# A hybrid attention block: PSUM as one tile with banks taken in turn by hand, and another order of steps at the last block's end

## The chip, the cores and the metric

The kernel runs on one core of one Trainium2 chip. The metric is the time of one execution on the device in microseconds (us). Its engines are named as in the profile: PE (TensorE, matmuls), DVE (VectorE), ACT (ScalarE), POOL (GpSimd) and SP (SyncE, here a queue for DMAs). PSUM, where matmuls leave their sums, has eight banks; one bank holds 128 rows of 512 fp32 numbers.

## The reference

One layer of a flow-matching backbone over 512 latent tokens of width 2048, with 256 context tokens:

```
h  = rmsnorm(x) * (1 + scale) + shift           # shift, scale, gate = silu(c) @ w_ada + b_ada
hc = the same of the context tokens
p  = h @ w_in                                   # 512 x 9216: q, k, v, z_a, u_b, z_b, g_a, g_b
q, k = rope(rmsnorm(heads)); kc, vc from hc @ w_in[:, k and v]
attn = softmax(q k^T) v                         # 12 heads over 4 k/v heads, 768 keys
y_a = (attn * silu(z_a)) @ w_proj_a
y_b = (fourier_2d(u_b) * silu(z_b)) @ w_proj_b
y   = (sigmoid(g_a) * y_a + sigmoid(g_b) * y_b) @ w_out
out = rmsnorm(x + gate * y) * final_g
```

All in fp32.

## The kernel before

Every fp32 product is made of three matmuls on halves of the numbers: each operand is split into a high part ("hi", rounded, by ACT, L163) and a low part ("lo", the difference, by DVE, L164), and `mm3` (L309) issues high times high, high times low and low times high (L311, L312, L313). The order of instructions on each engine is made by a planner, which models the time and takes, on each engine, the first instruction in program order whose inputs are ready; where the kernel says `issue_after` or `manual_schedule` it keeps the order written.

The stages, in order:

1. The start (to about 150 us): the modulation vectors (L492, a matrix-vector product whose weights are loaded while it runs), the normed tokens, and the products for the Fourier branch (`start_work`). It takes PSUM banks from a pool `ps` by three functions: `bank` (four buffers), `bank2` (two) and `bank3` (two). The Fourier transforms (`channels`, `positions`) use `bank`.
2. The projection groups (about 170 to 820 us): eight groups, of kinds qz, qz, qz, gate, gate, kv, gate, gate. A group makes a block of 1024 columns for all 512 tokens by seven products of a fast matrix scheme in place of eight: P1, Q5, P2, Q6, P7, Q3, Q4, in this order. A product comes in four pieces of weights, each with 12 matmuls, so 48 in all. P1 and P2 add up in one sum ("a"), Q5, Q6 and Q3 in a second ("b"), P7 and Q4 in a third ("c"). Each sum is a pair of banks. The second PSUM pool, `psp`, has two pairs under the tag "x" (for "a" and "c") and the pairs "y0" and "y1" (for "b"), taken by `pair`. The work at the end of a product takes pairs as well: in a qz group `pair("y")` at L906, `pair("x")` at L901 after P7 and `pair("y")` at L901 after Q3; in the kv group `pair("x")` at L916 after P2. At the end of Q4, DVE subtracts the sum "c" and the kept Q5 (L795, in `Group.run` L824), and the next group begins with P1. By Q5 of each group DVE also adds two loaded parts of its weights (L246).
3. Attention and the branch products (about 820 to 1180 us). Here the third pool, `psq`, is opened after `psp` is closed: one tile of all eight banks, with parts of it used by hand. `wide` are four stretches of one and a half banks over banks 0 to 5 for scores and transposes, bank 6 is for the `filler` (products that stand between those of the attention), bank 7 for the rest. Its first use is `fill(2)`: six matmuls into bank 6, then the first scores into `wide[1]`, that is the second half of bank 1 and bank 2.
4. The output projection (to the end): two groups of the same seven products. In the last one Q4 is done by `finish`: first the rows t=0, then t=1. For t=1 the last two of eight steps are done in column halves. `last` then weighs the sum with the gate, adds it to the rest, squares it with a running sum, and takes the root for the last norm; `Rms.scale` scales the four chunks of 512 columns and stores them.

A tile's users wait for each other by bank where it lies in PSUM. A new tile in a closed pool's place waits for all users of what lay there.

## Time and profile before

| | |
|---|---|
| median of 3 runs | 1321.96 us (1321.64 to 1322.66) |
| profiled execution | 1322.68 us |
| its span, first to last instruction | 1320.9 us |
| PE busy | 1297.7 us, 98% |
| DVE busy | 974.7 us, 74% |
| ACT busy | 652.7 us, 49% |
| POOL busy | 140.5 us, 11% |
| mean granted PE clock | 0.998 |

The span lies within the execution's time; 1.8 us lie around it. A line such as L313 is that of the helper `mm3`, so it stands for matmuls of all stages; what tells them apart is the name of the tile written: "pb", "pc", "pd" in the first pool, "x" and "y" in the second, "banks" in the third. In a timeline row the columns are the start and the length in us, the engine, the line, the operation, output<-inputs, the shape and the count, and in brackets the idle time before it and what ended it.

### The profile page before, as it was taken

What the parts mean: (1) busy time and instruction counts of PE and PEld (TensorE: products, weight loads), DVE (VectorE), ACT (ScalarE), POOL (GpSimd) and SP (SyncE); (2) the same over time, 40 slices, a digit from 0 to 9 for tenths busy, and PEclk for the clock granted to TensorE, in tenths of its full rate; (3) what the DMA queues carried; (4) which work ended last, traced back from release to release, by engine and by line L of the source; (5) the groups of instructions that cost most, each with busy time, mean ns of one, the idle gap of its engine ahead of it and who ended that gap; (6) DMA issues with size and microseconds to landing.
All of it is one profiled execution on the core that took longest, in us unless ns stands there. A gap on an engine that the chain in (4) does not pass through costs nothing.

```text
span 1320.9 us, 17489 instructions
## 1 busy us (share of the span) xinstructions
PE 1297.7 (98%) x6600; PEld 1062.3 (80%) x6600; DVE 974.7 (74%) x1290; ACT 652.7 (49%) x1019; POOL 140.5 (11%) x192
## 2 busy tenths in 40 slices
PE   7999999999999999999999999999999999999997
PEld 3577888888888888888888887888888888888885
DVE  4666899888777867746487666677776789777676
ACT  5222655555555554444354454666666133355544
POOL 0110011110201111011021110000000100111210
PEclk9999999999999999999999999999999999999999
DMA  9898587887898988977669886122013899678985
GB/s 382 330 371 340 175 243 196 226 233 219 205 318 196 276 280 244 297 166 190 193 167 303 235 245 217 45 72 81 33 65 112 321 332 329 186 175 222 225 208 170
DMA packets 96085, 291.28 MB, mean 221 GB/s; under 512 B 8960, under 2 KB 32000, under 8 KB 91648
## 3 DMA queue, kind: packets, MB, share of 16 engines
q1 hardware_dynamic: 48576, 163.65, 35.5%
q0 software_dynamic: 22800, 96.49, 30.7%
q10 hardware_dynamic: 24624, 30.02, 6.6%
q8 instruction: 52, 0.85, 0.3%
q14 instruction: 33, 0.27, 0.1%
HBM read 263.37 MB, written 26.75 MB: 220 GB/s over the span
## 4 chain that ended last, share of the span: by engine, by line
PE 96%; DMA 1%; ACT 1%; DVE 1%; issue 0%; SPq 0%; DVEq 0%; ACTq 0%
PE banks L311 11%; PE banks L312 11%; PE banks L313 11%; PE x L312 9%; PE x L313 9%; PE x L311 9%; PE y L312 8%; PE y L311 8%; PE y L313 8%; PE banks L1201 3%; PE pd L492 2%; PE pb L311 2%; PE pb L313 1%; PE pb L312 1%; PE pc L311 1%; PE pc L313 1%
## 5 line engine op out<-in xcount | busy, mean ns | idle before, releaser
L163 ACT ACTIVATE whi<-wr 128x1024 fp32r<-128x1024 f32 (+1 forms) x129 | 135.1, 1051 | 161.5 <-PE banks L313 91.8
L164 DVE TENSOR_TENSOR wlo<-wr,whi 128x1024 fp32r<-128x1024 f32 (+1 forms) x129 | 155.8, 1211 | 53.8 <-ACT whi L163 53.5
L164 DVE TENSOR_TENSOR wlo<-R,whi 128x1024 fp32r<-128x1024 f32 x114 | 138.5, 1221 | 65.7 <-ACT whi L163 65.4
L163 ACT ACTIVATE whi<-R 128x1024 fp32r<-128x1024 f32 x114 | 120.3, 1059 | 131.5 <-PE x L313 37.2
L311 PE MATMUL banks<-whi,s 128*128 128x512 f32 (+1 forms) x422 | 166.2, 394 | 1.7 <-DVE ev L795 1.5
L312 PE MATMUL banks<-wlo,s 128*128 128x512 f32 (+1 forms) x422 | 165.0, 391 | 0.0
L313 PE MATMUL banks<-whi,s 128*128 128x512 f32 (+1 forms) x422 | 164.5, 390 | 0.0
L311 PE MATMUL x<-whi,s 128*128 128x512 f32 x352 | 137.2, 390 | 0.0
L313 PE MATMUL x<-whi,s 128*128 128x512 f32 x352 | 137.0, 389 | 0.0
L312 PE MATMUL x<-wlo,s 128*128 128x512 f32 x352 | 137.0, 389 | 0.0
L311 PE MATMUL y<-whi,s 128*128 128x512 f32 x316 | 123.1, 389 | 0.0
L312 PE MATMUL y<-wlo,s 128*128 128x512 f32 x316 | 123.0, 389 | 0.0
L313 PE MATMUL y<-whi,s 128*128 128x512 f32 x316 | 122.8, 389 | 0.0
L267 POOL DMA_DIRECT2D R<-in_w_g x64 | 55.3, 865 | 421.5 <-DVE wlo L164 224.0
L163 ACT ACTIVATE s<-wr 128x512 fp32r<-128x512 f32 (+2 forms) x93 | 61.3, 678 | 65.9 <-PE y L312 16.3
L311 PEld LDWEIGHTS banks<-whi,s 128*128 128x128 f32 x422 | 79.3, 188 | 17.8 <-ACT whi L163 1.9
L313 PEld LDWEIGHTS banks<-whi,s 128*128 128x128 f32 x422 | 79.3, 188 | 16.3
L312 PEld LDWEIGHTS banks<-wlo,s 128*128 128x128 f32 x422 | 79.4, 188 | 14.8
L164 DVE TENSOR_TENSOR s<-wr,s 128x512 fp32r<-128x512 f32 (+2 forms) x93 | 67.1, 747 | 22.0 <-ACT s L163 20.8
L311 PEld LDWEIGHTS x<-whi,s 128*128 128x128 f32 x352 | 66.1, 188 | 13.7
L312 PEld LDWEIGHTS x<-wlo,s 128*128 128x128 f32 x352 | 66.1, 188 | 13.7 <-DVE wlo L164 0.2
L313 PEld LDWEIGHTS x<-whi,s 128*128 128x128 f32 x352 | 66.1, 188 | 13.6
(279 smaller groups left out, 2766.4 us busy)
## 6 DMA issues: line engine op xcount, KB each, us to landing
wr<-in_w_g SPq DMA_DIRECT2D x128, 512.0 KB, 5.1
R<-in_w_g POOLq DMA_DIRECT2D x64, 512.0 KB, 6.7
wa<-in_w_ss POOLq DMA_DIRECT2D x26, 1024.0 KB, 8.0
R<-in_w_g SPq DMA_DIRECT2D x32, 512.0 KB, 5.4
wr<-in_w_pab SPq DMA_DIRECT2D x32, 512.0 KB, 5.3
wr<-in_w_gate SPq DMA_DIRECT2D x32, 512.0 KB, 5.7
wr<-in_w_o SPq DMA_DIRECT2D x24, 512.0 KB, 6.7
R<-in_w_o POOLq DMA_DIRECT2D x24, 512.0 KB, 8.1
```

What stands on the lines that cost most here:

```text
L163: first = nc.scalar.activation(hi, src, ACT.Copy)
L164: return first, nc.vector.tensor_tensor(lo, src, hi.bitcast(F32), op=ALU.subtract)
L267: nc.gpsimd.dma_start(chain[e.pc], e.nxt, accum_op=ALU.add)
L311: nc.tensor.matmul(o, ah, bh, start=start, stop=False, skip_group_check=cont)
L312: nc.tensor.matmul(o, ah, bl, start=False, stop=False, skip_group_check=cont)
L313: nc.tensor.matmul(o, al, bh, start=False, stop=stop, skip_group_check=cont)
L492: last = nc.tensor.matmul(acc[32 * j : 32 * j + 32, :256], c2[:, kk, :], w[:, k, :], start=kk < 4, stop=kk >= KK - 4)
L1201: nc.tensor.transpose(tp[:, k * P : (k + 1) * P], p[:, k * P : (k + 1) * P], ident)
```

## The change

PSUM becomes one tile of eight banks, `whole_psum`, at the start of the kernel. `bank`, `bank2` and `bank3` take banks 0 to 3, 4 to 5 and 6 to 7 of it, each in strict turn. `pair` takes pairs in strict turn too, "x" from banks 0 to 3 and "y" from banks 4 to 7, where the second pool had tags with buffers. The closing of the first two pools goes. In `finish`, t=1 is done like t=0, in whole widths. In `last`, the weighing is one instruction for 512 columns; for t=1 the sum over the squares leaves out the last one (`rest`), which goes into the root as its input (`root_of`), with the sum of the others as its bias; and chunk 3 is scaled and stored in two halves (`scale_part`).

```diff
-    pss, ps = region("ps", None, space=PSUM)
+
+    psq = ctx.enter_context(tc.tile_pool(name="psq", bufs=1, space=PSUM, reuse_waits="tile"))
+    whole_psum = psq.tile([P, 8, 512], F32, name="banks")
+    turn_b = [0, 0, 0]
+
+    def next_bank(i, first, n):
+        turn_b[i] += 1
+        return whole_psum[:, first + (turn_b[i] - 1) % n, :]
...
-    def bank(shape=(P, 512)):
-        return ps.tile(list(shape), F32, tag="b1", bufs=4, name=uid("pb"))
+    def bank():
+        return next_bank(0, 0, 4)
 
     def bank2():
-        return ps.tile([P, 512], F32, tag="b2", bufs=2, name=uid("pd"))
+        return next_bank(1, 4, 2)
 
     def bank3():
-        return ps.tile([P, 512], F32, tag="b3", bufs=2, name=uid("pc"))
+        return next_bank(2, 6, 2)
...
-    pss.close()
...
-    pgs, psp = region("psp", None, space=PSUM, reuse_waits="tile")
-    last_y = [0]
-
-    banks = []
+    last_y = [0, 1]
...
     def pair(tag, skip=0):
-        if banks:
-            last_y[tag == "x"] += 1
-            b = 2 * (last_y[tag == "x"] % 2) + (4 if tag == "y" else 0)
-            return banks[0][:, b : b + 2, :] if b < 6 else banks[1]
-        if tag == "y":
-            last_y[0] += 1 + skip
-            return psp.tile([P, 2, 512], F32, tag=f"y{last_y[0] % 2}", bufs=1, name=uid(tag))
-        return psp.tile([P, 2, 512], F32, tag=tag, bufs=2, name=uid(tag))
+        last_y[tag == "x"] += 1 + skip
+        b = 2 * (last_y[tag == "x"] % 2) + (4 if tag == "y" else 0)
+        return whole_psum[:, b : b + 2, :]
...
             w = []
             for t in range(2):
-                for j in range(8 - 2 * t):
+                for j in range(8):
...
                     self.mm(a, form, j, t, w[j // 2], False, j == 7, cont=True)
-                if t:
-
-                    for c in (slice(0, 256), slice(256, 512)):
-                        for j in (6, 7):
-                            ah, al = (v[:, P:] for v in self.forms[form][j])
-                            mm3(a[:, t, c], ah, al, w[3][0][:, j % 2, c], w[3][1][:, j % 2, c], False, j == 7, cont=True)
                 self.last(self.Y, a, t)
...
-    pgs.close()
-    psq = ctx.enter_context(tc.tile_pool(name="psq", bufs=1, space=PSUM, reuse_waits="tile"))
-    whole_psum = psq.tile([P, 8, 512], F32, name="banks")
-    banks += [whole_psum[:, :6, :], whole_psum[:, 6:, :]]
+    banks = [whole_psum[:, :6, :], whole_psum[:, 6:, :]]
     last_y[:] = [0, 0]
...
+        def rest(self):
+            nc.vector.tensor_reduce(self.r[:, 0:1], ssq[:, self.t, 0:4], axis=AX.X, op=ALU.add)
+            nc.vector.tensor_scalar(self.r[:, 0:1], self.r[:, 0:1], 1.0 / D, EPS, op0=ALU.mult, op1=ALU.add)
+
+        def root_of(self, i):
+            nc.scalar.activation(self.r[:, 1:2], ssq[:, self.t, i : i + 1], ACT.Sqrt, bias=self.r[:, 0:1], scale=1.0 / D)
+
+        def scale_part(self, j, parts):
+
+            v, r = o[self.t // 2, j][:, self.t % 2, :], self.r[:, 1:2]
+            for c, _ in parts:
+                nc.scalar.mul(v[:, c], v[:, c], r)
+                nc.sync.dma_start(out[self.t * P : (self.t + 1) * P, 512 * j + c.start : 512 * j + c.stop], v[:, c])
...
-        def weigh(c):
-            nc.vector.tensor_tensor(tmp[:, c], a[:, t, c], gates[0][:, 0, c], op=ALU.mult)
-
-        def add(c, i):
-            nc.vector.tensor_tensor(Y[:, t, c], tmp[:, c], Y[:, t, c], op=ALU.add)
-            squares_of(Y[:, t, c], 2 + t, i)
-
         r = Rms(2 + t)
         with tc.manual_schedule(engines={mybir.EngineType.DVE, mybir.EngineType.Activation}):
+            nc.vector.tensor_tensor(tmp, a[:, t, :], gates[0][:, 0, :], op=ALU.mult)
             for c, i in half:
-                weigh(c)
-                add(c, i)
-            r.add()
-            r.root()
+                nc.vector.tensor_tensor(Y[:, t, c], tmp[:, c], Y[:, t, c], op=ALU.add)
+                squares_of(Y[:, t, c], 2 + t, i)
+            if t:
+
+                r.rest()
+                r.root_of(4)
+            else:
+                r.add()
+                r.root()
             r.turn()
-            r.scale(3, True)
+            if t:
+                r.scale_part(3, half)
+            else:
+                r.scale(3, True)
             r.scale(1)
```

## The prediction

> **What bounds the kernel now.** I read the page first (busy shares and the chain), then the waits of TensorE, then the windows by stage, then the timeline at the places that the change touches.

> ```profile
> PE 1297.7 (98%) x6600; PEld 1062.3 (80%) x6600; DVE 974.7 (74%) x1290; ACT 652.7 (49%) x1019; POOL 140.5 (11%) x192
> ...
> PE 96%; DMA 1%; ACT 1%; DVE 1%; issue 0%; SPq 0%; DVEq 0%; ACTq 0%
> ```

> TensorE is busy for 98% of the span and is 96% of the chain that ended last. So a stall of TensorE costs its length, and only what it waits for now can be won. The waits of TensorE, and the windows (columns: length; busy us of PE, PEld, DVE, ACT, POOL with counts; granted clock; DMA share; GB/s):

> ```profile
> PE banks L311 <- DVE ev L795: 1.5, 1, 1.5
> ```
> ```profile
> 25.00:140.00 115.00, 114.45 (x838) 76.53 (x837) 72.77 (x142) 31.88 (x48) 14.15 (x26) 1.00 0.87 337
> 240.00:815.00 575.00, 575.00 (x2544) 475.98 (x2544) 416.25 (x496) 288.54 (x465) 70.49 (x81) 1.00 0.82 233
> 815.00:840.00 25.00, 23.53 (x135) 20.10 (x134) 14.88 (x23) 13.80 (x21) 0.53 (x1) 1.00 0.29 108
> 840.00:1060.00 220.00, 218.72 (x1381) 189.56 (x1380) 163.65 (x268) 124.30 (x214) 10.53 (x20) 1.00 0.32 111
> 1311.60:1315.20 3.60, 0.00 (x0) 0.00 (x0) 2.50 (x7) 1.90 (x6) 0.00 (x0) 1.00 0.70 261
> 1315.30:1320.90 5.60, 0.00 (x0) 0.00 (x0) 0.72 (x2) 0.64 (x2) 0.00 (x0) 0.50 0.51 187
> ```

> From 240 to 815 us (the projection groups) TensorE never idles: 2544 matmuls in 575 us, 0.226 us from one to the next, so a product of 48 takes 10.85 us. The PSUM pools cost one visible wait, 1.5 us, where the third pool opens at 820 us. The first stage loses 0.55 us in 115 with DMA at 0.87, so by-hand banks have little to win there.

> **The change part by part.**

> *The pool boundary at 820 us.* One tile from the start means that a matmul waits for the last readers of its own bank, not of all eight.

> ```profile
> 819.83 0.39 PE L313 MATMUL x<-whi,s 128*128 128x512 f32 x1
> 821.69 0.47 PE L311 MATMUL banks<-whi,s 128*128 128x512 f32 x1 [1.47 <-DVE ev L795]
> 822.00 0.40 PE L312 MATMUL banks<-wlo,s 128*128 128x512 f32 x1
> 822.23 0.40 PE L313 MATMUL banks<-whi,s 128*128 128x512 f32 x1
> ```
> ```profile
> 820.26 1.29 DVE L795 TENSOR_TENSOR ev<-x,ev 128x512 f32<-128x512 f32 x2 [0.40 <-PE x L313]
> ```

> Unhindered, the third matmul would start at 819.83+3x0.226=820.51 instead of 822.23: 1.72 us are lost, of which 0.09 is the slow restart (0.54 for two steps instead of 0.45). After the change the first six matmuls (the filler, bank 6) wait for nothing, since bank 6 held the "b" sum that ended with Q3. They take 1.36 us, to 821.42. The scores that follow write the second half of bank 1 and bank 2; of these only bank 2 holds the sum of Q4, and its half of the subtraction is done by about 820.9. So the wait goes. What is late next is the softmax:

> ```profile
> 823.05 1.28 ACT L1185 ACT_TABLE_LOAD   x1 [0.41 <-ACT ev L850]
> 825.41 0.91 ACT L1185 ACTIVATE s<-banks,gain 128x768 f32<-128x768 f32 x1 [1.08 <-DVE gain L1183]
> ```

> The table load hangs on ScalarE's own queue and ends at 824.33 whatever TensorE does, so the first exponential moves by 825.41-824.33=1.08 us at most. Gain between 1.08 and 1.72; I take 1.5, since the later stage idles only 1.28 us in 220 and so has matmuls to put in between.

> *The turn of the "x" pairs.* Before, "x" is a tag with two buffers and a sum gets the one that is free; "y" alternated by name already. After, "x" strictly alternates too: odd turns are banks 2-3, even ones 0-1. Counting calls in a "qz" group: the "a" sum of P1 (turn 2, banks 0-1), the "c" sum of P7 (turn 3, banks 2-3), the tanh of the second half at L901 (turn 4, banks 0-1). Three are an odd number, so P1 of the next group is turn 5: banks 2-3, where the "c" sum of the Q4 just ended still waits for DVE's subtraction at L795. The same happens from the second to the third group and from the third to the first "gate" group. "gate" groups take two turns, the "kv" group three of which the last is P7's own, so it is not met again. Now the three places as they are:

> ```profile
> 248.15 1.22 DVE L795 TENSOR_TENSOR ev<-x,ev 128x1024 f32<-128x1024 f32 x1
> ...
> 323.78 1.22 DVE L795 TENSOR_TENSOR ev<-x,ev 128x1024 f32<-128x1024 f32 x1
> ...
> 400.18 1.22 DVE L246 TENSOR_TENSOR R<-R,wr 128x1024 f32<-128x1024 f32 x1
> 401.32 1.22 DVE L795 TENSOR_TENSOR ev<-x,ev 128x1024 f32<-128x1024 f32 x1
> 402.46 1.21 DVE L164 TENSOR_TENSOR wlo<-R,whi 128x1024 fp32r<-128x1024 f32 x1
> ```
> ```profile
> 248.21 0.39 PE L313 MATMUL x<-whi,s 128*128 128x512 f32 x1
> ...
> 257.95 0.39 PE L311 MATMUL y<-whi,s 128*128 128x512 f32 x1
> ...
> 334.11 0.39 PE L311 MATMUL y<-s,s 128*128 128x512 f32 x1
> ...
> 410.27 0.39 PE L311 MATMUL y<-whi,s 128*128 128x512 f32 x1
> ```

> The "y" rows are the first matmuls of Q5, so P1 began 10.85 us earlier: 247.10, 323.26, 399.42. At 248.21 it writes "x" while DVE reads "x": it has the other buffer. In the strict turn it starts when the subtraction has ended, with the 0.14 us between DVE's end (821.55) and the matmul (821.69) at the pool boundary, and the restart of 0.09. The losses are 249.37+0.23-247.10=2.50, 325.00+0.23-323.26=1.97 and 402.54+0.23-399.42=3.35, in all 7.8 us. The subtraction does not come at once because DVE is at other work (L246 in the third case). If it did, it would start 0.43 us after the last matmul's start, as at 820.26, and each stall would be 0.43-0.23+1.22+0.23=1.65, three 4.95 us.

> What could stand in the stall? Everything behind P1 on TensorE: matmuls of Q5's first piece write "y" and could go ahead.

> ```profile
> 399.65 1.06 ACT L163 ACTIVATE whi<-R 128x1024 fp32r<-128x1024 f32 x1 [1.67 <-PE x L313]
> ```
> ```profile
> 138.39 0.39 PE L311 MATMUL pc<-s,whi 128*128 128x512 f32 x1
> 138.83 1.21 PE L311 MATMUL pb<-s,whi 128*128 128x512 f32 x4
> ```

> That single matmuls are put ahead where others wait is seen at 138.39. But Q5's weights get their buffer only when Q4 is done (ScalarE waits for "PE x L313"), the high part is ready at 400.71 and the low part at 403.67, behind the subtraction. So the first matmul for each of two banks can go ahead, 0.45 us a stall. Bounds of the cost: 4.95-1.35=3.6 and 7.8. I take 7.8-1.35=6.5, as the rows of the three places themselves are the nearest. The stalls come in a stretch with no idle time, so nothing behind gives them back.

> A long stall could also cost clock. In the windows above TensorE has nothing to do from 1311.6 on, its clock stays 1.00 to 1315.2 and is 0.50 after: 3.6 us of idleness were borne. The longest stall here, 3.35, is just below. [...]

> *The end.* PE: twelve half matmuls become six whole ones.

> ```profile
> 1311.14 0.28 PE L312 MATMUL banks<-wlo,s 128*128 128x256 f32 x1
> 1311.26 0.28 PE L313 MATMUL banks<-whi,s 128*128 128x256 f32 x1
> 1311.58 0.42 DVE L1494 TENSOR_TENSOR s<-banks,s 128x256 f32<-128x256 f32 x1 [0.54 <-PE banks L313]
> ...
> 1312.56 0.42 ACT L1405 ACTIVATE s<-s 128x256 f32<-128x256 f32 x1 [1.59 <-DVE s L1497]
> ...
> 1313.35 0.42 ACT L1405 ACTIVATE s<-s 128x256 f32<-128x256 f32 x1 [0.29 <-DVE s L1497]
> 1313.67 0.19 ACT L1405 ACTIVATION_READ_ACCUMULATOR s<-s 128x1 f32 x1
> 1313.89 0.16 DVE L1468 TENSOR_REDUCE r<-ssq 128x1 f32<-128x5 f32 x1 [0.64 <-ACT s L1405]
> 1314.08 0.29 ACT L1471 ACTIVATE r<-r,eps_t 128x1 f32<-128x1 f32 x1 [0.22 <-DVE r L1468]
> ...
> 1314.61 1.34 ACT L1481 ACTIVATE s<-s,r 128x512 f32<-128x512 f32 x2 [0.23 <-DVE r L1474]
> ```

> Twelve half matmuls 0.12 apart end 11x0.12+0.28=1.60 after the first one's start, six whole ones 5x0.226+0.39=1.52 after it: 0.08 won. The halving did not let DVE begin early: 1311.58 is after all matmuls, so giving it up costs nothing there. One weighing of 512:

> ```profile
> 1299.95 0.69 DVE L1428 TENSOR_TENSOR s<-banks,s 128x512 f32<-128x512 f32 x1 [2.55 <-PE banks L313]
> 1300.68 0.69 DVE L1429 TENSOR_TENSOR s<-s,s 128x512 f32<-128x512 f32 x1
> ```

> It takes 0.73 to the next step instead of 0.46, so the first squares start 0.27 later; the second then run on ScalarE's queue, one step (0.32+0.19+0.03=0.54) behind the first: 0.98+0.27+0.54=1.79 after the start of weighing, against 1.77 now. Even. Then the sum (1313.89) falls out of the chain: the root starts right after the accumulator is read (1313.86) instead of at 1314.08, 0.2 won. The sum of the other four squares and its scaling lie on DVE beside the second squares. The scaling in halves lets the first store leave 0.67-0.42=0.25 earlier; it adds one store ahead of the others on SP's queue, worth between -0.2 and +0.25; I take 0.1. The end: 0.08+0.2+0.1=0.4 won, bounds 0 to 0.6.

> **The sum.** +6.5-1.5-0.4=+4.6 us. The profiled execution took 1322.68 us (span 1320.9 and 1.8 around it), so 1327.3; the median of the runs shown is 0.72 less, so 1326.6. With the bounds the least is +3.6-1.72-0.6=+1.3, the most +7.8-1.08=+6.7; the order of instructions in the first 170 us may shift by a microsecond either way, as the planner sees other waits.

> **The rivals.** *The stalls are filled (other side).* If the planner puts all of Q5's first piece, 12 matmuls of 0.226 or 2.7 us, ahead of P1, the first two stalls vanish and 0.6 is left of the third: 0.6-1.5-0.4=-1.3, 1320.7. It decides from the moment when both parts of that piece are ready before the subtraction ends. For it: the reordering at 138.39. Against: the low part's row, 402.46, stands behind the subtraction.

> *Only the floor.* If DVE reaches the subtraction at once, since the first stall lets it run ahead, the cost is 2.50+2x1.65=5.8, less 1.35: 4.45-1.9=+2.5, 1324.5.

> *Clock.* If the third stall halves the clock for as long as the idle time that triggers it, 3.6 us, another 1.8 is lost: +6.4, 1328.4. [...]

> *No new wait.* If the strict turn gives the same pairs as the buffers did, the stalls fall away, and the wins of 1.9 remain: 1320.1. My count of turns speaks against it.

> **How the numbers follow.** Forecast 0.58, floor 0.17, clock 0.06, filled 0.12, no new wait 0.07. The range from 1322.5 to 1329.0 leaves out the last two, mostly, and takes in the bounds of the stalls. A measurement can tell about 0.2% or 2.6 us from no change. Slower by more than that: forecast 0.54 of its 0.58, clock, and half of the floor, 0.69. Within: most of filled and no new wait, the rest of the floor, 0.25. Faster: a shift of the first stage on top of the last two, 0.06.

> **What would show it.** Right: TensorE's waits list three waits of P1 ("banks L311" on DVE's L795) of 1.5 to 3.2 us near 248, 326 and 404 us; the wait near 820 us is gone; the root follows the last accumulator read by 0.03 us. Wrong: TensorE stays busy for 575 of 575 us from 240 to 815, or Q5's matmuls stand between Q4 and P1 in the timeline.

## The result: 12 us slower, and the profile after

| | before | after |
|---|---|---|
| median | 1321.80 us (1321.43 to 1322.66, 6 runs) | 1334.11 us (1329.78 to 1336.91, 6 runs) |
| ratio | | 1.0087 [1.0077, 1.0098] |
| profiled execution, span | 1322.68, 1320.9 us | 1336.91, 1335.1 us |
| mean granted clock of the profiled run | 0.998 | 0.993 |

The prediction said 1326.6 us and at most 1329.0. The sign was right, the size was not. After the change the early helper lines stand 7 lower in the file (L311 to L313 are L318 to L320, L163 and L164 are L170 and L171, L246 is L253), and the subtraction L795 is L793.

The page after, first the busy engines, then the chain that ended last:

```profile
PE 1303.6 (98%) x6594; PEld 1065.2 (80%) x6594; DVE 976.1 (73%) x1289; ACT 651.6 (49%) x1020; POOL 139.3 (10%) x192
...
PE 87%; DVE 5%; DMA 3%; ACT 2%; issue 2%; SPq 0%; POOL 0%; ACTq 0%; DVEq 0%
```

TensorE is still busy for 98%, but it is busy for 6 us more with the same work: it ran at a lower clock for part of it (a mean of 0.993 for 0.998). Its share of the chain fell from 96% to 87%. The waits of TensorE that are new (in us: total, times, longest) and the projection groups by window:

```profile
PE banks L318 <- DVE ev L793: 5.9, 2, 3.5
PE banks L318 <- ACT whi L170: 2.6, 2, 1.4
PE banks L319 <- DVE wlo L171: 1.8, 1, 1.8
```
```profile
240.00:815.00 575.00, 564.68 (x2461) 464.81 (x2460) 408.53 (x487) 280.41 (x457) 68.22 (x79) 0.99 0.80 226
```

Where 575.00 of 575 us were busy, 10.3 are idle now. The wait of 1.5 us at 820 us has no row any more. The timeline of TensorE has the idle times at three places, of which the first two were forecast:

```profile
245.47 0.39 PE L320 MATMUL banks<-whi,s 128*128 128x512 f32 x1
247.06 0.73 PE L318 MATMUL banks<-whi,s 128*128 128x512 f32 x2 [1.20 <-ACT whi L170]
250.12 0.50 PE L318 MATMUL banks<-whi,s 128*128 128x512 f32 x1 [2.33 <-DVE ev L793]
...
403.88 0.39 PE L320 MATMUL banks<-whi,s 128*128 128x512 f32 x1
405.69 0.73 PE L318 MATMUL banks<-whi,s 128*128 128x512 f32 x2 [1.42 <-ACT whi L170]
409.95 0.79 PE L318 MATMUL banks<-s 128*128 128x512 f32 x1 [3.52 <-DVE ev L793]
...
690.28 0.50 PE L319 MATMUL banks<-wlo,s 128*128 128x512 f32 x1 [1.76 <-DVE wlo L171]
```

Two matmuls of Q5 go ahead, as forecast, and then P1 waits for the subtraction. Behind each of the three places the clock falls to half (third column from the right):

```profile
252.00:254.00 2.00, 2.00 (x6) 1.53 (x5) 1.97 (x6) 0.55 (x4) 1.63 (x3) 0.50 0.65 119
...
410.00:412.00 2.00, 2.00 (x5) 1.61 (x6) 2.00 (x3) 2.00 (x15) 0.67 (x1) 0.50 0.64 248
...
692.00:694.00 2.00, 2.00 (x6) 1.54 (x6) 2.00 (x2) 0.00 (x0) 1.48 (x2) 0.50 1.25 302
```

In these windows a matmul comes every 0.43 us instead of 0.226. Added up over the windows, the clock is at half for 3.4, 6.8 and 3.4 us.

### The profile page after: what moved, and what is told of

It reads as the page before. It is cut to its first block, busy times and chain, and to the rows that moved or that the text cites. A ratio compares the mean times of both kernels' runs of the same rounds, so it can differ in the third digit from the quotient of the medians.

```text
span 1335.1 us, 17449 instructions
## 1 busy us (share of the span) xinstructions
PE 1303.6 (98%) x6594; PEld 1065.2 (80%) x6594; DVE 976.1 (73%) x1289; ACT 651.6 (49%) x1020; POOL 139.3 (10%) x192
## 3 DMA queue, kind: packets, MB, share of 16 engines
q1 hardware_dynamic: 48720, 163.65, 34.9%
## 4 chain that ended last, share of the span: by engine, by line
PE 87%; DVE 5%; DMA 3%; ACT 2%; issue 2%; SPq 0%; POOL 0%; ACTq 0%; DVEq 0%
PE banks L318 27%; PE banks L319 27%; PE banks L320 27%; PE banks L1190 3%; PE banks L499 2%; DVE wlo L171 1%; DMA R<-in_w_g 1%; DMA wa<-in_w_ss 1%; DMA wr<-in_ctx_toks 1%; DVE s L171 1%; DVE ev L793 1%; ACT banks L878 1%; DVE R L253 0%; PE banks L1291 0%; PE banks L1205 0%
## 5 line engine op out<-in xcount | busy, mean ns | idle before, releaser
L318 PE MATMUL banks<-whi,s 128*128 128x512 f32 x1088 | 426.8, 393 | 5.2 <-ACT whi L170 2.6
L319 PE MATMUL banks<-wlo,s 128*128 128x512 f32 x1088 | 426.6, 392 | 1.8 <-DVE wlo L171 1.8
L320 PE MATMUL banks<-whi,s 128*128 128x512 f32 x1088 | 425.7, 391 | 0.0
L318 PEld LDWEIGHTS banks<-whi,s 128*128 128x128 f32 x1088 | 204.6, 188 | 48.3 <-ACT whi L170 3.5
L319 PEld LDWEIGHTS banks<-wlo,s 128*128 128x128 f32 x1088 | 205.2, 189 | 43.5 <-DVE wlo L171 2.6
L320 PEld LDWEIGHTS banks<-whi,s 128*128 128x128 f32 x1088 | 205.2, 189 | 42.9
L170 ACT ACTIVATE whi<-wr 128x1024 fp32r<-128x1024 f32 (+1 forms) x129 | 135.0, 1051 | 164.6 <-PE banks L320 144.2
L171 DVE TENSOR_TENSOR wlo<-wr,whi 128x1024 fp32r<-128x1024 f32 (+1 forms) x129 | 156.1, 1214 | 58.0 <-ACT whi L170 57.6
L171 DVE TENSOR_TENSOR wlo<-R,whi 128x1024 fp32r<-128x1024 f32 x114 | 139.0, 1222 | 72.5 <-ACT whi L170 72.3
L170 ACT ACTIVATE whi<-R 128x1024 fp32r<-128x1024 f32 x114 | 120.2, 1059 | 143.1 <-PE banks L320 120.1
L319 PE MATMUL banks<-s,s 128*128 128x512 f32 (+1 forms) x440 | 168.2, 383 | 0.1
L320 PE MATMUL banks<-s,s 128*128 128x512 f32 (+1 forms) x440 | 166.8, 381 | 0.0
L318 PE MATMUL banks<-s,s 128*128 128x512 f32 (+1 forms) x430 | 166.1, 388 | 0.5 <-ACT s L170 0.5
L318 PEld LDWEIGHTS banks<-s,s 128*128 128x128 f32 x430 | 81.3, 189 | 18.6 <-ACT s L170 1.1
L319 PEld LDWEIGHTS banks<-s,s 128*128 128x128 f32 x440 | 83.4, 189 | 15.8 <-DVE s L171 0.5
L320 PEld LDWEIGHTS banks<-s,s 128*128 128x128 f32 x440 | 83.0, 189 | 15.4
L170 ACT ACTIVATE s<-wr 128x512 fp32r<-128x512 f32 (+2 forms) x93 | 61.9, 679 | 65.3 <-PE banks L320 25.6
L171 DVE TENSOR_TENSOR s<-wr,s 128x512 fp32r<-128x512 f32 (+2 forms) x93 | 67.4, 751 | 30.3 <-ACT s L170 30.1
L170 ACT ACTIVATE s<-R 128x512 fp32r<-128x512 f32 (+1 forms) x84 | 55.2, 669 | 41.2 <-PE banks L320 29.6
L171 DVE TENSOR_TENSOR s<-R,s 128x512 fp32r<-128x512 f32 (+1 forms) x84 | 60.4, 739 | 17.4 <-ACT s L170 17.3
L259 DVE TENSOR_TENSOR wr<-R,wr 128x1024 f32<-128x1024 f32 x40 | 48.9, 1221 | 17.2 <-DMA wr<-in_w_g 10.9
```

The source lines that it names most:

```text
L170: first = nc.scalar.activation(hi, src, ACT.Copy)
L171: return first, nc.vector.tensor_tensor(lo, src, hi.bitcast(F32), op=ALU.subtract)
L259: nc.vector.tensor_tensor(src, chain[e.pc], src, op=ALU.subtract)
L318: nc.tensor.matmul(o, ah, bh, start=start, stop=False, skip_group_check=cont)
L319: nc.tensor.matmul(o, ah, bl, start=False, stop=False, skip_group_check=cont)
L320: nc.tensor.matmul(o, al, bh, start=False, stop=stop, skip_group_check=cont)
```

## The experiments

All times are medians beside runs of the kernel before on the same chip; the interval is that of the ratio.

| kernel | time | before | ratio |
|---|---|---|---|
| strict turn alone | 1329.81 us | 1322.15 | 1.0062 [1.0047, 1.0077] |
| change + spare turn | 1323.52 us | 1322.15 | 1.0012 [1.0003, 1.0020] |
| change + subtraction ahead of additions | 1335.21 us | 1322.15 | 1.0095 [1.0082, 1.0108] |
| change + subtraction ahead of all | 1329.15 us | 1322.08 | 1.0060 [1.0046, 1.0074] |
| change + filling matmuls | 1334.51 us | 1322.15 | 1.0092 [1.0077, 1.0107] |
| change + later rotation | 1332.19 us | 1322.73 | 1.0073 [1.0059, 1.0087] |
| change + spare turn + later rotation | 1321.05 us | 1322.08 | 0.9993 [0.9985, 1.0002] |
| the same again | 1320.71 us | 1322.73 | 0.9987 [0.9979, 0.9996] |
| end alone | 1322.11 us | 1322.08 | 1.0001 [0.9992, 1.0010] |
| both edits + held gaps | 1345.69 us (2 runs) | 1322.08 | 1.0179 [1.0160, 1.0197] |
| both edits + held gaps of 1.6 to 1.9 us | 1343.19 us (2 runs) | 1322.73 | 1.0156 [1.0138, 1.0175] |

"Both edits" are the spare turn and the later rotation.

**The turn: done alone, and undone.** The theory was that the strict turn of three makes P1 wait and that the rest follows from it; the rival, that the one tile makes the planner order everything worse. The kernel before with the turn alone:

```
-        return psp.tile([P, 2, 512], F32, tag=tag, bufs=2, name=uid(tag))
+        turn_x[0] += 1
+        return psp.tile([P, 2, 512], F32, tag=f"x{turn_x[0] % 2}", bufs=1, name=uid(tag))
```

> The kernel before with one edit: the two buffers of the tag "x" become two tags with one buffer each, taken in strict turn, as "y" had it; three pools, the end as before. Theory (the turn alone makes the loss): waits of P1 on the subtraction near 248 and 400 us as in the changed kernel, with half clock behind them, and the wait of 1.5 us at 820 us still there: 1322 + 5.7 + 0.4 + 7.9, about 1336, and 1332 if the loss near 690 us does not come. Rival (the loss comes from the one tile): 1321 to 1323.

The changed kernel with one more turn counted in each qz group:

```
             e = pair("x" if half else "y")
+            last_y[1] += half
```

> The changed kernel, with one more turn of the "x" pairs counted at the end of each qz group (a qz group then takes an even number, four, and P1 of the next group gets the pair that the sum "c" of Q4 does not hold). Theory (the strict turn of three makes P1 wait for the subtraction, and the half clock and the later loss before the sixth group follow from it): the waits of P1 on the subtraction at 247 and 405 us are gone, no half clock from 240 to 700 us, and what is left is the gain at 820 us (about 1.9), that of the end (0.3) and that of the start (1.3): 1318.5 to 1319.5 us. If only the two waits go and the loss of 3.9 us near 690 us stays, 1322 to 1323. Rival (one tile instead of three pools makes the planner order the whole kernel worse, and the turn is incidental): 1328 or more.

The turn alone costs 6.2 to 10.2 us by its interval. Its trace has P1 wait at the same two places, though for less: 3.4 us in all, where the changed kernel has 5.9. The one line of the spare turn takes 10.6 us off the median of the changed kernel. What TensorE still waits for in the projection groups, in the trace of the version with the spare turn:

```profile
PE banks L319 <- DVE wlo L171: 1.8, 1, 1.8
```

So the theory holds for the two forecast places, and its end, that the loss near 690 us follows from them, falls: with the spare turn the wait of 1.76 us is still there, now at 676 us. The wait near 690 us is not in the turn alone, for which 1332 was expected without it; that the median lies below even that goes with the shorter waits of P1, and with a higher clock in four of its six runs.

The turn alone also gives the clock's price. Its six runs fall into two at a mean clock of 0.993 (1334.65 and 1333.50 us) and four at 0.997 (1328.05 to 1330.24): the same program, 5.1 us apart in the means. As far as the mean clock tells (none of the four was profiled), these show what the waits cost by themselves: 6 to 8 us, beside the 6.5 forecast.

**The length of the waits.** First VectorE's additions to Q5's raw weights were put behind the subtraction, then the low-part splits of P1 and Q5 too:

```
+        with ExitStack() as line:
+            if e.key[0] == "Q5" and e.key[1] in (1, 2, 3):
+                line.enter_context(tc.issue_after(q4_sub[-1].ins))
+            for r in raws:
+                nc.vector.tensor_tensor(src, src, r, op=ALU.add)
...
+                if not in_q4[0] and e.key[0] in ("P1", "Q5") and e.key[1] in (1, 2, 3):
+                    line.enter_context(tc.issue_after(q4_sub[-1].ins))
                 last_split.append(split_from(src, hi, lo))
```

> The changed kernel, with VectorE's additions to the raw weights of Q5 (L253) in the second to fourth group put behind the subtraction at the end of the group before, which was queued behind them (it ended 4.6 and 6.0 us after Q4's last matmul began). Theory (the queue of VectorE, not the turn alone, made the waits longer than the floor of 1.65 us, and long enough for the clock to halve): waits of 1.2 to 1.9 us each, half clock gone or shorter; Q5's weights come up to 2.3 us later, which the 10.85 us of P1 cover: 1323 to 1326. Rival (the additions are not what counts; the subtraction is late for the products' sake): 1333 to 1335.

> The run before (the subtraction ahead of the additions to Q5's weights) left two low-part splits ahead of the subtraction at the third place, and the wait there was 4.81 us; at the other two it fell to 1.41, the floor. Now these splits (P1's and Q5's, in the second to fourth group) stand behind the subtraction too. Theory (the length of each wait is VectorE's queue, and a wait of 1.4 us does not halve the clock): three waits of 1.4 us, three losses of 1.65 us, no half clock from 240 to 420 us, and so 4.95 us on top of the version with the spare turn: 1323.5 + 5 = 1328.5 us. Rival (the waits halve the clock whatever their length, or the splits that were put back are late for P1): 1331 or more.

The first missed its time by 9 us: two splits were left ahead of the subtraction at the third place, where the wait grew to 4.81 us. TensorE's timeline of the first, with two waits at the floor and the third at 4.81, and of the second, with three at the floor:

```profile
247.67 0.47 PE L322 MATMUL banks<-whi,s 128*128 128x512 f32 x1 [1.41 <-DVE ev L797]
325.49 0.47 PE L322 MATMUL banks<-whi,s 128*128 128x512 f32 x1 [1.41 <-DVE ev L797]
406.71 0.77 PE L322 MATMUL banks<-s 128*128 128x512 f32 x1 [4.81 <-DVE ev L797]
```
```profile
245.61 0.39 PE L326 MATMUL banks<-whi,s 128*128 128x512 f32 x1
247.41 0.47 PE L324 MATMUL banks<-whi,s 128*128 128x512 f32 x1 [1.41 <-DVE ev L800]
...
325.24 0.47 PE L324 MATMUL banks<-whi,s 128*128 128x512 f32 x1 [1.41 <-DVE ev L800]
...
403.08 0.47 PE L324 MATMUL banks<-s 128*128 128x512 f32 x1 [1.41 <-DVE ev L800]
```

From 245.61+0.23 to 247.41 are 1.57 us, with the slow restart the 1.65 that the prediction had as floor. In the trace of the second no window of 2 us between 240 and 700 us has a clock under 0.99, and its median is 5.6 us above that of the version with the spare turn, for 4.95 expected. So the length of each wait is VectorE's queue ahead of the subtraction, and waits of 1.41 us did not halve the clock in these two traces. Three of the five runs of the second took 1329 to 1332 us at a mean clock of 0.996 to 0.997; none of them was profiled, so what lowered the clock there is not shown.

**The clock.** Matmuls that nothing reads were put into two of the waits, 12 and 20 of them:

```
+        for _ in range({1: 12, 3: 20}.get(g, 0)):
+            nc.tensor.matmul(whole_psum[:, 2 * ((last_y[0] + 1) % 2) + 4, :], hhi[15][:, :P], hhi[15], start=True, stop=True)
```

> The changed kernel with 12 matmuls of 512 columns more after Q4 of the first group and 20 after Q4 of the third, into a bank that is free there; nothing reads their result. They take 12 x 0.226 = 2.7 and 20 x 0.226 = 4.5 us, less than or about what TensorE stands idle there (1.20 + 2.33 and 1.42 + 3.52 us), so the start of P1 moves by less than 1 us. Theory (the idle gap halves the clock, and that costs on top of the wait): the half clock of 3.3 and 6 us behind the two waits goes, 1.7 + 2.5 = 4 us faster than the changed kernel, about 1330. Rival (the clock drop is no more than a mark of the idle time, or comes anyway): 1334 to 1335.

The half clock behind the two places went, and its profiled run (1332.61 us) is 4.3 us under that of the changed kernel, about the 1.7 + 2.45 that the clock took there. But its median is that of the changed kernel. The four runs all have a clock of 0.997; three of them took 2 us more than the profiled one, and no trace shows where. This experiment does not settle the price of the clock; the two groups of the turn alone do.

What the clock does behind idle times of different lengths was then measured by itself. On the version with the spare turn and the later rotation, TensorE is held at the seven borders between the groups:

```
+                if name == "P1" and g:
...
+                    nc.tensor.matmul(spare, junk, junk[:, :8], start=True, stop=True)
+                    for _ in range(GAPS[g]):
+                        nc.gpsimd.memset(junk, 0.0)
+                    held = nc.tensor.matmul(spare, junk, junk[:, :8], start=True, stop=True)
+                if name in ("P1", "Q5") and g:
+                    line.enter_context(tc.issue_after(held.ins))
```

> The clock's answer to a gap by itself. The version with the spare turn and the later rotation steps, and at each of the seven borders between the projection groups TensorE is held: a small matmul reads a tile, GpSimd then writes it 1, 3, 5, 7, 9, 11 and 13 times over, and a second small matmul reads it again, before which neither P1 nor Q5 may start. Nothing reads their result. The gaps should come out at some 0.6 to 4 us. [...] Rival (the row of the prediction: up to 3.6 us of idle time are borne): no half clock behind any gap under 3.6 us.

TensorE's timeline (the bracket is the gap), and the windows in which the clock first falls:

```profile
402.52 0.39 PE L1135 MATMUL banks<-junk 128*128 128x8 f32 x2 [1.38 <-POOL junk L1134]
481.68 0.50 PE L1135 MATMUL banks<-junk 128*128 128x8 f32 x2 [1.90 <-POOL junk L1134]
562.59 0.39 PE L1135 MATMUL banks<-junk 128*128 128x8 f32 x2 [2.48 <-POOL junk L1134]
684.25 0.59 PE L1135 MATMUL banks<-junk 128*128 128x8 f32 x2 [2.95 <-POOL junk L1134]
767.22 0.39 PE L1135 MATMUL banks<-junk 128*128 128x8 f32 x2 [3.47 <-POOL junk L1134]
```
```profile
480.00:482.00 2.00, 0.32 (x2) 0.32 (x3) 2.00 (x4) 1.46 (x3) 1.28 (x7) 0.96 0.34 102
562.00:564.00 2.00, 1.42 (x7) 1.17 (x8) 1.97 (x3) 1.06 (x1) 0.42 (x3) 0.94 0.76 256
682.00:684.00 2.00, 0.00 (x0) 0.00 (x0) 2.00 (x4) 2.00 (x16) 1.54 (x9) 0.80 0.06 20
768.00:770.00 2.00, 2.00 (x7) 1.61 (x6) 0.00 (x0) 0.00 (x0) 0.07 (x1) 0.64 1.03 277
```

Behind 0.33, 0.85 and 1.38 us the clock stayed: the matmuls of P1 came 0.23 us apart. With the four longer gaps it halved, so the reading of the prediction's row, that 3.6 us are borne, was wrong. A mean of 0.96 over 2 us means 0.16 us at half, so the half clock began at 481.84; in the same way at 563.76, 683.20 and 768.56. That is 0.16, 1.17 and 1.34 us after the end of the gaps of 1.90, 2.48 and 3.47 us, and 1.05 us before the end of the one of 2.95, which had 1.32 us of other idle time just ahead of it. The matmuls then came 0.43 us apart up to 485.16, 566.90, 689.96 and 771.82, so the clock was at half for at least 3.3, 3.1, 6.8 and 3.3 us. The same with gaps between 1.38 and 1.90 us:

> The held borders again, with 6, 7, 6, 7, 6, 7, 6 writes, so gaps of about 1.64 and 1.90 us by the steps of the run before (0.26 us a write). [...]

```profile
248.51 0.39 PE L1135 MATMUL banks<-junk 128*128 128x8 f32 x2 [1.63 <-POOL junk L1134]
328.82 0.39 PE L1135 MATMUL banks<-junk 128*128 128x8 f32 x2 [1.89 <-POOL junk L1134]
...
564.98 0.39 PE L1135 MATMUL banks<-junk 128*128 128x8 f32 x2 [1.69 <-POOL junk L1134]
```
```profile
248.00:250.00 2.00, 1.49 (x7) 1.27 (x8) 2.00 (x2) 0.00 (x0) 0.40 (x2) 0.88 0.88 272
```

Behind the first gap, 1.63 us, the clock was at half from 249.52 on, for 3.4 us. Behind the gaps of 1.89 us at 328 us and of 1.69 at 565 us it stayed at 1.00. Of the seven, only the first and the one near 684 us halved it, the latter for 6.8 us; that is a gap of 1.89 us that had 1.32 us of other idle time just ahead of it. Two more gaps of 1.63 us and one more of 1.89 left it at 1.00. So between these lengths the gap's length alone does not tell what the clock does. The bracket of a held gap leaves out the small matmuls of 8 columns at its ends, which the view shows as 0.28 and 0.39 us of busy time; whether they matter to the clock is not shown. The waits near 680 us, which have no such matmuls, do not agree with each other either. In the changed kernel the wait of 1.76 us halved the clock, from 691.36 on; so did the same wait with the filling matmuls (1.77) and with the subtraction ahead of the additions (1.76). With the subtraction ahead of all it did not:

```profile
682.09 0.50 PE L325 MATMUL banks<-wlo,s 128*128 128x512 f32 x1 [1.77 <-DVE wlo L171]
```
```profile
682.00:684.00 2.00, 1.91 (x8) 1.59 (x9) 2.00 (x4) 0.00 (x0) 0.53 (x1) 1.00 1.13 276
```

In these traces, then, held gaps of up to 1.38 us and single waits of 1.41 us left a full clock full, and held gaps of 1.90 us or more were all followed by half; between 1.63 and 1.89 us both came, and what decides there is open.

**The loss near 690 us.** VectorE's timeline of the changed kernel there, and that of the kernel before at the same work:

```profile
685.54 1.21 DVE L885 TENSOR_TENSOR qr<-qr,banks 128x1024 f32<-128x1024 f32 x1
...
687.87 1.22 DVE L886 TENSOR_TENSOR qr<-qr,small 128x1024 f32<-128x1024 f32 x1
689.01 2.35 DVE L171 TENSOR_TENSOR wlo<-R,whi 128x1024 fp32r<-128x1024 f32 x2
```
```profile
673.41 2.35 DVE L164 TENSOR_TENSOR wlo<-R,whi 128x1024 fp32r<-128x1024 f32 x2
...
679.26 1.21 DVE L893 TENSOR_TENSOR qr<-qr,y 128x1024 f32<-128x1024 f32 x1
```

Q5's low parts stand behind the last two steps of the kv group's rotation, where they stood ahead of them. These two steps were put two pieces later (for the kv group's second half; its stores with them). The edit also closes the pool `qzs` and opens `gvp` one product later, behind P1 of the next group; that was not tried apart:

```
+        if then:
+            jobs.extend([lambda: None, lambda: None, rest])
```

> The version with the spare turn, and the last two steps of the rotation of the kv group's second half (L885, L886), with their stores, written out two pieces later, behind the splits of the next group's Q5, as VectorE had them in the kernel before. Theory (in the one tile ScalarE takes all eight squares in a row, so these steps are ready early and go ahead of the splits that TensorE waits for near 676 us): the wait of 1.76 us near 676 us goes, with the 0.3 of slow restart and the half clock that follows it in part of the runs: 2 to 3 us faster than the version with the spare turn, 1320 to 1321.5 us, and runs that lie within 1 us of each other. Rival (the weights are late for another reason, such as the loads or ScalarE): 1323 to 1324.

> The changed kernel with the later rotation steps alone, so with the strict turn of three. Theory (the losses are separate and add up: the turn with its half clock 10.6 us, the rotation steps 2.5): 1334.1 - 2.5 = 1331.6 us, and in the trace the waits of 247 and 405 us with half clock behind them, and none near 690. Rival (the loss near 690 us came from the delay of the turn, and is gone or larger without it): 1334, or under 1330.

> The version with the spare turn and the later rotation steps once more, unchanged, beside the kernel before: it came out 1.0 us faster, with an interval that just holds no change. If the one tile's gain at 820 us and the 0.4 us of the end are real and nothing is left over: 1.0 to 1.9 us faster, 1320.2 to 1321.1. If the first value was chance: within 0.3 us of before.

The wait went, and the windows of the version with both edits are full again:

```profile
240.00:815.00 575.00, 574.68 (x2541) 474.83 (x2540) 415.33 (x496) 283.94 (x465) 72.48 (x81) 1.00 0.80 233
```

With the turn left strict the loss that remains is 9.5 us by medians, so the later rotation is worth 2.8 of the 12.3; with the spare turn it is worth 2.9 (from 1.4 above before to 1.5 under it). The order of the rotation is a cause of its own. With both edits the kernel is faster than before, by 1.0 us with an interval that holds no change, and in the second measurement by 0.5 to 2.8 us: it beats the changed kernel in both, and the kernel before clearly in one. Why the planner has these steps ready earlier in the one tile (ScalarE takes the eight squares in a row there, and in two parts before) was not tried apart.

**The end alone**, the change's edits of `finish`, `Rms` and `last` in the kernel before.

> The kernel before with the change of the end alone (whole widths in finish, one weighing, the last squares straight into the root, chunk 3 scaled and stored in halves). Theory (the end is worth what the prediction summed, 0.4 us, and the root follows the last accumulator read by 0.03 us): 0.3 to 0.4 us faster than before, 1321.8 beside 1322.15, hardly to be told from no change. Rival (the extra store and the longer queue of ScalarE eat it): 0 to 0.3 us slower.

No difference within 1.3 us either way, so the 0.4 stays unproved as a time. In the traces the stretch behind 1282 us of the kernel before, in which the end lies, is shorter by 0.4 us with the end alone, in the changed kernel and with both edits, but by 0.05 in the version with the spare turn.

## Why the prediction was wrong

The sum of the change by the medians: the turn with its clock 11.0 us (beside the later rotation, 9.5 above before with it and 1.5 under before without it, the mean of two measurements), the rotation 2.8 (12.3 less 9.5), and 1.5 won by the rest: 12.3. These close by construction, as differences of rows of the table. The two profiled runs, 14.2 us apart, give the sum by place, from how far the subtractions L793 lie behind those of the kernel before: 1.4 won ahead of the first place (the prediction allowed a microsecond either way there), 5.7 lost at the first, 8.2 at the second and third, 0.2 up to 680 us, 3.7 near 690, 1.9 won by 1202 us and 0.4 at the end. Of the 17.6 lost at the four places, 5.9 are clock. Forecast was 6.5 - 1.5 - 0.4.

- **The count of turns** was right: P1 waits for L793 at the first and third place, and one spare turn undoes it.
- **The second place** took the rival of the filled stall. The step "Q5's weights get their buffer only when Q4 is done" was read off one place and used for three. Here eight matmuls of Q5 go ahead of P1, on weights in "s" slots that had been split early, the first and the last of them and P1 itself being:

```profile
327.58 0.61 PE L318 MATMUL banks<-s,s 128*128 128x512 f32 x2
...
329.30 0.62 PE L318 MATMUL banks<-s,s 128*128 128x512 f32 x2
329.76 0.39 PE L318 MATMUL banks<-whi,s 128*128 128x512 f32 x1
```

  Of the 2.18 us the eight take 1.81, and only 0.37 are lost for the 1.52 forecast.
- **The size of the other stalls** was too small, 4.0 and 5.4 us for 2.05 and 2.90 (P1's start, less Q4's end and the two matmuls put ahead). The failed step took the distance between P1 and the subtraction as it was before. But TensorE and VectorE's queue do not move together: at the first place Q4's last matmul began 1.4 us earlier (245.47 for 247.10-0.23), the subtraction 0.7 later (248.85 for 248.15). At the third, ScalarE and VectorE of the changed kernel:

```profile
398.70 0.63 ACT L170 ACTIVATE s<-R 128x512 fp32r<-128x512 f32 x1 [3.19 <-DMA R<-in_w_g]
399.24 1.01 ACT L894 ACTIVATE banks<-ev 128x1024 f32<-128x1024 f32 x1
```
```profile
400.28 1.23 DVE L895 SCALAR_TENSOR_TENSOR ev<-banks,ev 128x1024 f32<-128x1024 f32 x1 [0.77 <-ACT banks L894]
...
408.68 1.22 DVE L793 TENSOR_TENSOR ev<-banks,ev 128x1024 f32<-128x1024 f32 x1
```

  The tanh stands behind a split that waited for a load, and from VectorE's use of it to the subtraction are 8.40 us of queue. In the kernel before it was the same chain with the same queue:

```profile
391.36 0.63 ACT L163 ACTIVATE s<-R 128x512 fp32r<-128x512 f32 x1 [1.95 <-DMA R<-in_w_g]
```
```profile
392.94 1.23 DVE L903 SCALAR_TENSOR_TENSOR ev<-y,ev 128x1024 f32<-128x1024 f32 x1 [0.98 <-ACT y L902]
```

  From 392.94 to the subtraction at 401.32 are 8.38 us. So the queue is no longer than it was: the split behind the load came 7.34 us later, but Q4's last matmul only 4.7 (403.88 for 399.42-0.23). Why the load came later by more than TensorE did is not shown. The rival "only the floor" was the other way out, and the runs reach it only when that queue is put in order.
- **The clock** was the gravest step: it was put at nothing, and took 5.9 us of the profiled run, which is the slowest of the six. (The fastest, 1329.78 us at 0.997, is above the range even so.) "3.6 us of idleness were borne" was the wrong reading of a right row: the clock is at 0.50 in the window that begins at 1315.3, so that idle time too was followed by half clock, and with the held gaps 1.90 us were enough. Two waits halved the clock for 1.7 and 2.45 us of loss in the profiled run, and the wait near 690 for 1.7 more. The rival had a chance of 0.06. A stall of 3.35 us was taken for one that is borne; near 690 us a wait of 1.76 was not.
- **The loss near 690 us** was not in the prediction at all. It allowed for another order of instructions in the first 170 us alone, and the planner's other view of the waits acted where it made no allowance.
- **The pool boundary** went as forecast: no wait near 820, and between 808 and 1202 us the profiled run makes up 1.9 us for the 1.5 forecast.
- **The end**: the root follows the read by 0.03 us, as forecast:

```profile
1328.20 0.19 ACT L1394 ACTIVATION_READ_ACCUMULATOR s<-s 128x1 f32 x1
1328.42 0.29 ACT L1464 ACTIVATE r<-ssq,r 128x1 f32<-128x1 f32 x1
```

## What to carry to other kernels

When buffers are turned by hand, count the turns of one whole loop pass: an odd number over two buffers hands the next pass the one still being read, and here one spare turn did better (1323.5 us) than putting the releaser's queue in order (1329.2). Size a new wait from both chains, that of the waiter and that of the releaser's queue, since an edit moves them apart. Where one engine never idles, ask for each new idle time not only how long it is, but whether the clock is at half behind it (here it was behind one wait of 1.76 us and not behind another of 1.77); and after a change of buffers compare the order on the other engines all along, not only at the edit.
